# A second expert matrix split between a dense and a gathered product: 896 and 1152 columns instead of 1024 and 1024

## The chip, the cores and the metric

The kernel runs on one core of a Trainium2 chip. A core has five engines with instruction streams of their own: TensorE (PE, matrix products, with the loading of weights shown apart as PEld), VectorE (DVE), ScalarE (ACT), GpSimd (POOL) and SyncE (SP), which here only issues transfers. Sixteen DMA engines move data between the chip's memory (HBM) and the core's memory (SBUF); matrix products land in PSUM, eight banks of 512 fp32 numbers for each of 128 partitions. The metric is the device time of one execution in microseconds (us), the median of several; lower is better.

## What is computed

Two transformer blocks on 256 tokens of width 2048, in fp32. The change lies in the second block's expert layer. Each token gets 128 of 16384 experts with a weight each (eight heads, the sixteen best of each); expert e has a row of 2048 numbers in `expert_u` and one in `expert_v`:

```
def block(args):
    xb, ib, gb = args                 # tokens, their 128 expert indices, their 128 gates
    act = jax.nn.gelu(jnp.einsum('tkd,td->tk', expert_u[ib], xb))
    return jnp.einsum('tk,tkd->td', act * gb, expert_v[ib])
...
h = h + peer(rms_norm_2(h, ffn_norm_gain[i]), w_pq[i], sub_k1[i], sub_k2[i], expert_u[i], expert_v[i])
gate = jax.nn.sigmoid(rms_norm_2(h, ple_norm_gain[i]) @ w_ple_gate[i])
h = h + gate * (p[i] @ w_ple_proj[i])
```

## The kernel before

Every engine executes its instructions in the order in which the program writes them. That order comes out of a main line of code and of five lanes, generators that are stepped beside it: `lanes.step()` takes one step in each lane, `step_one(4)` one in lane 4 alone.

Weights come in chunks of 128 x 1024 numbers, 512 KB each, into four buffers `raw` (L335), issued on SP's queue in a fixed order. `next_chunk` releases the chunk just used, issues the load that takes its buffer, and steps the lanes once. Most weights are split into two parts by ACT (L349) and DVE (L350); the expert weights are used whole.

The expert layer has these pieces. First `u_rows` (lane 4) gathers, for each of 256 slots, the 128 rows of `expert_u` that the tokens ask for (two times 128 slots for two tiles of 128 tokens; L1663, 8 KB a row), and DVE multiplies them with the tokens and sums (L1703). The rows stand in seats of the slabs `rows`; with the second tile only four seats are used.

Then the product with `expert_v` is made in two ways, each for a part of its 2048 columns:

- Gathered, `w_vs`: `v_rows` (lane 4) gathers a row for each of 128 tokens per slot (256 gathers) into seats `vrow`, which are pieces of the first two `rows` slabs, and DVE multiplies by the slot's weight and adds into `sacc` in PSUM (L1838 for a tile's first slot, L1840 for the others). A step of the lane issues up to two gathers, if their seats are free, and writes one accumulation. After 128 slots ACT copies `sacc` out (L1847), and `turned` lets PE transpose it by blocks into the PSUM tile `tok` (L1815), from where DVE adds it to `x` (L1817).
- Dense, `w_vd`: a matrix G with one row for each of the 16384 experts and one column for each token holds the weights. `spots` builds it, eight tokens at a time, as products of two indicator matrices P and Q (L1762, L1794), which ACT copies out (L1745). Then 128 chunks of 128 experts are multiplied on PE (L1900) and summed in four PSUM banks `accv`. For the second tile of tokens the half with the lower experts is built before this loop (PSUM tile `sp`), the other half beside its first 62 chunks (PSUM tile `tok`).

The loop over the chunks takes two steps of lane 4 for each chunk: one inside `next_chunk`, one with `step_one(4)`. Ahead of the second stands a small copy on POOL that reads the chunk, so POOL goes on only when the chunk has landed:

```
for j in range(8):
    w, _ = next_block()
    if j == 0:
        G.tensor_copy(xb["beat"], w[:, 0:1])
        lanes.step_one(4)
    o = ps[j // 2][:, (j % 2) * T:(j % 2) * T + T]
    PE.matmul(o, w, gs_[k // 16][:, k % 16], ...)
```

Behind the loop the four banks are added to `x` (L1904), the blocks of `x` are squared and split (`x_block`), the projections `w_pp` and `w_pg` follow, and the result is stored.

Of the kernel before, what the change touches and what calls it, by code (L numbers as in the profile page):

```python
# [6 lines left out]
F32 = mybir.dt.float32  # L7
# [8 lines left out]
T = 256  # L16
D = 2048
DFF = 5632
NEG = -1.0e30
CH = 1024  # L20
GORD = [3, 2, 1, 0]
HORD = [0, 4, 1, 5, 2, 6, 3, 7]

# [40 lines left out]
def layout(i):  # L64

    a = {}
# [43 lines left out]
    a["w_pq"] = blocks(i["w_pq_2"][0])  # L110
    a["subk"] = np.ascontiguousarray(np.stack([i["sub_k1_2"][0], i["sub_k2_2"][0]], axis=1).transpose(3, 0, 1, 2)).reshape(128, 2048)
    a["w_u"] = np.ascontiguousarray(i["expert_u_2"][0])
    a["w_vd"] = np.ascontiguousarray(i["expert_v_2"][0][:, :CH])
    a["w_vs"] = np.ascontiguousarray(i["expert_v_2"][0][:, CH:])
    a["w_pg"] = blocks(i["w_ple_gate_2"][0])
    a["w_pp"] = blocks(i["w_ple_proj_2"][0])
    a["pt"] = np.ascontiguousarray(i["p_2"][0, 0].T.reshape(2, 128, T).transpose(1, 0, 2))
# [108 lines left out]
def program(tc, A, out, stage=99, dbg=None):  # L226
# [62 lines left out]
    def bank(p, name):  # L289
        return p.tile([128, 512], F32, name=name, tag="bank")  # L290
# [26 lines left out]
    if stage > 3:  # L317
        add("w_pq", split=False)
        whole.update(range(len(order), len(order) + 128))
        add_kout("w_vd", 128, 0)  # L320
    if stage > 4:
        add("w_pp"); add("w_pg")

# [1199 lines left out]
    def pair(name):  # L1523

        return pairs_[name].tile([128, 1024], F32, name=name, tag="pair")
# [190 lines left out]
    def spots(tt):  # L1716
# [50 lines left out]
        else:  # L1767

            for half in range(2):
                lo, p = half * 64, None  # L1770
                for n in range(16):
# [15 lines left out]
                            yield  # L1787
                    else:
                        G.tensor_mul(Pn, Pn, wT[:, ts][:, :, None].to_broadcast(narrow))
                    if half == 0 or n % 2 == 0:  # L1790
                        p = pair("tok" if half else "sp")
                    at = 0 if half == 0 else n % 2 * 512
                    for k in range(8):
                        PE.matmul(p[:, at + k * 64:at + k * 64 + 64], Q[:, k], P[:, k, 0:64], start=True, stop=True)  # L1794
                    if half:
                        yield
                    if half and n % 2:
                        put(range(4, 8), t0 - 8, p, 16)
                    elif not half:
                        put(range(4), t0, p[:, 0:512], 8)  # L1800
                    yield
                flags[("g", 1, half)] = True
        flags[("g", tt)] = True


    vrow = [t.rearrange("p n d -> p (n d)").rearrange("p (n d) -> p n d", n=4)[:, j] for t in rows_[:2] for j in range(4)]
# [12 lines left out]

    def v_rows():  # L1820
        while not flags.get("u"):
            yield
        m, busy = 0, {}
        sacc = None
        for n in range(256):
            tt, s = divmod(n, 128)
            for _ in range(4 if n == 0 else 1):
                for _ in range(2):
                    if m < 256 and m % 8 not in busy:
                        gather(vrow[m % 8], A["w_vs"], m)  # L1830
# [4 lines left out]
            r, w = vrow[n % 8], wv[:, tt, s:s + 1]  # L1835
# [5 lines left out]
            del busy[n % 8]  # L1841
            if s == 127:
                if tt:
                    t = vrow[1]
                else:
                    t = gs_["t"] = hip.tile([128, CH], F32, name="tok", tag="whi")
# [31 lines left out]
    for k in range(128):  # L1878
# [11 lines left out]
        if k == 84:  # L1890
            for j in range(2):
                part(pl[:, 0, j], pl[:, 1, j], pf[:, j], None)
        for j in range(8):
            w, _ = next_block()
            if j == 0:

                G.tensor_copy(xb["beat"], w[:, 0:1])
                lanes.step_one(4)
            o = ps[j // 2][:, (j % 2) * T:(j % 2) * T + T]
            PE.matmul(o, w, gs_[k // 16][:, k % 16], start=(k == 0 and j % 2 == 0), stop=k == 127, skip_group_check=True)  # L1900
    x, xh, xl = xb["x"], xb["h"], xb["l"]

    for i, q_ in enumerate(ps):
        V.tensor_add(x[:, 2 * i:2 * i + 2], x[:, 2 * i:2 * i + 2], q_.rearrange("p (k t) -> p k t", t=T))  # L1904
    for j in range(8):
        x_block(j, x, C("ple"), xh, xl)
    gt5 = xb["c"](4, T)
    pl = xb["p"]
# [4 lines left out]

    project(16, 2, (pl[:, 0], pl[:, 1]), pp_done)
    until("v")
    for j in range(8, 16):
        x_block(j, x, C("ple"), xh, xl)
    psum_close(3)
    accp, bgN = psum("accz", 4), psum("bgz", 1)
# [35 lines left out]
```

## Time and profile before

| | us |
|---|---|
| median of three runs | 2967.11 |
| lowest, highest | 2965.75, 2971.43 |
| profiled execution | 2963.08 |
| its span, first to last instruction | 2961.3 |
| PE, PEld, DVE busy | 2311.8, 2106.1, 1999.7 |
| ACT, POOL busy | 1191.2, 900.9 |

The profile is one execution. Busy times are sums over the span, so a share is a mean over stages with different limits; the stage that the change touches lies between about 2270 and 2870 us. PEclk is the granted clock of TensorE, 1.00 for 2.4 GHz and 0.50 for 1.2 GHz. The DMA share is the mean busy share of the sixteen DMA engines.

### The profile page before, as it was taken

The numbers are of one execution on the slowest core, as the hardware profiler recorded it, in microseconds if no ns is written. First come the engines' busy times: TensorE is split into PE (matmuls) and PEld (weight loads), VectorE is DVE, ScalarE is ACT, GpSimd is POOL, SyncE is SP. The second block draws the span as 40 slices with busy tenths as digits, with TensorE's granted clock in tenths as the row PEclk, the third lists the DMA queues.
The fourth block names the chain that finished last, engine by engine and source line by source line (L and its number), as shares of the span: only waits on it lengthen the run. The fifth ranks groups of instructions, "written<-read, shape, count | busy, mean of one in ns | idle before, by whom it ended". The sixth has DMA issues, their size and how long they took to land.

```text
span 2961.3 us, 39499 instructions
## 1 busy us (share of the span) xinstructions
PE 2311.8 (78%) x14635; PEld 2106.1 (71%) x14635; DVE 1999.7 (68%) x2615; ACT 1191.2 (40%) x2560; POOL 900.9 (30%) x1262
## 2 busy tenths in 40 slices
PE   8999999999999999999997200022222999999799
PEld 8887898888889999998986200011122988888689
DVE  5455666555556565656537999988998866666655
ACT  4355555444444454445411000058880444400043
POOL 3202215111111000331135543333334555555420
PEclk9999999999999999999998655555555799999999
DMA  6444455655655555543557799999997799999945
GB/s 221 153 128 122 134 158 180 196 188 187 197 187 190 185 180 184 172 151 109 182 201 279 291 407 422 422 397 408 415 415 317 265 403 404 395 401 409 366 148 166
DMA packets 174675, 765.11 MB, mean 258 GB/s; under 512 B 19585, under 2 KB 22049, under 8 KB 141201
## 3 DMA queue, kind: packets, MB, share of 16 engines
q1 hardware_dynamic: 99216, 353.83, 36.0%
q0 software_dynamic: 75264, 408.75, 34.5%
q8 instruction: 115, 1.88, 0.3%
q14 instruction: 80, 0.65, 0.1%
HBM read 757.77 MB, written 4.21 MB: 257 GB/s over the span
## 4 chain that ended last, share of the span: by engine, by line
PE 59%; DMA 12%; DVE 10%; issue 9%; POOL 8%; ACT 1%; another core or an unknown queue 0%; SPq 0%; POOLq 0%; DVEq 0%; ACTq 0%
PE acc L411 11%; PE acc L1900 7%; PE acc L386 6%; PE acc L388 6%; PE acc L387 6%; DMA rows<-w_vs,idx 6%; PE acc L412 6%; POOL rows L1663 5%; DMA rows<-w_u,idx 5%; DVE rows L1703 5%; PE acc L485 3%; PE acc L483 3%; PE acc L484 3%; PE sp L1794 1%; DMA raw<-w_vd 1%
## 5 line engine op out<-in xcount | busy, mean ns | idle before, releaser
L350 DVE TENSOR_TENSOR wlo<-raw,whi 128x1024 fp32r<-128x1024 f32 (+1 forms) x501 | 613.5, 1233 | 415.1 <-ACT whi L349 408.3
L349 ACT CAST whi<-raw 128x1024 fp32r<-128x1024 f32 (+1 forms) x501 | 519.7, 1042 | 380.2 <-PE acc L387 130.9
L1703 DVE SCALAR_TENSOR_TENSOR rows<-rows,yt 128x2048 f32<-128x2048 f32 x256 | 580.3, 2285 | 42.9 <-DMA rows<-w_u,idx 38.6
L1900 PE MATMUL acc<-G,raw 128*128 128x256 f32 x2048 | 457.3, 385 | 12.4 <-DMA raw<-w_vd 11.1
L1900 PEld LDWEIGHTS acc<-G,raw 128*128 128x128 f32 x2048 | 391.8, 193 | 71.7 <-DMA raw<-w_vd 17.0
L1840 DVE SCALAR_TENSOR_TENSOR sacc<-rows,sm,sacc 128x1024 f32<-128x1024 f32 x254 | 327.3, 1289 | 143.8 <-DMA rows<-w_vs,idx 127.4
L1663 POOL DMA_INDIRECT rows<-w_u,idx x256 | 244.2, 954 | 380.0 <-DVE rows L1703 274.8
L1663 POOL DMA_INDIRECT rows<-w_vs,idx x256 | 248.8, 972 | 149.6 <-DVE sacc L1840 81.7
L411 PE MATMUL acc<-xl,whi 128*128 128x512 f32 x704 | 248.2, 391 | 0.0
L411 PE MATMUL acc<-xh,whi 128*128 128x512 f32 x704 | 248.1, 391 | 0.0
L1762 PE MATMUL sp<-P,Q 128*128 128x128 f32 x256 | 60.2, 430 | 213.9 <-ACT P L1758 213.9
L1762 PEld LDWEIGHTS sp<-P,Q 128*128 128x128 f32 x256 | 55.8, 330 | 218.6 <-ACT P L1758 218.6
L564 POOL TENSOR_TENSOR acc_sq<-acc_sq,sq 128x256 f32<-128x256 f32 x63 | 57.0, 904 | 504.6 <-ACT sq L563 502.7
L485 PE MATMUL acc<-ring,wlo 128*128 128x256 f32 x704 | 199.3, 283 | 0.1
L483 PE MATMUL acc<-ring,whi 128*128 128x256 f32 x704 | 199.3, 283 | 0.1
L484 PE MATMUL acc<-ring,whi 128*128 128x256 f32 x704 | 199.2, 283 | 0.0
L412 PE MATMUL acc<-xh,wlo 128*128 128x256 f32 x704 | 197.2, 280 | 0.0
L412 PE MATMUL acc<-xl,wlo 128*128 128x256 f32 x704 | 197.1, 280 | 0.0
L1659 PE MATMUL yt<-keep,xg 128*128 128x128 f32 x32 | 5.6, 350 | 237.6 <-DVE rows L1703 237.1
L1191 POOL TENSOR_TENSOR hT<-cF 128x256 f32<-128x256 f32 x44 | 70.8, 1609 | 372.7 <-ACT whi L349 342.8
L1659 PEld LDWEIGHTS yt<-keep,xg 128*128 128x128 f32 x32 | 5.0, 184 | 238.1 <-DVE rows L1703 237.3
L386 PE MATMUL acc<-xh,whi 128*128 128x256 f32 x520 | 150.6, 290 | 3.2 <-ACT whi L349 1.8
(486 smaller groups left out, 5692.7 us busy)
## 6 DMA issues: line engine op xcount, KB each, us to landing
raw<-w_gu SPq DMA_DIRECT2D x176, 512.0 KB
raw<-w_vd SPq DMA_DIRECT2D x128, 512.0 KB
raw<-w_down SPq DMA_DIRECT2D x88, 512.0 KB
raw<-w_out SPq DMA_DIRECT2D x32, 512.0 KB
raw<-w_pq SPq DMA_DIRECT2D x32, 512.0 KB
raw<-w_pg SPq DMA_DIRECT2D x32, 512.0 KB
raw<-w_b SPq DMA_DIRECT2D x24, 512.0 KB
raw<-w_lat SPq DMA_DIRECT2D x18, 512.0 KB
```

Of the source, the lines that this page charges most:

```text
L349: S.copy(hi[j][:, a:b], raw[j][:, a:b])
L350: V.tensor_sub(lo[j][:, a:b], raw[j][:, a:b], hi[j][:, a:b].bitcast(F32))
L386: PE.matmul(ps, wh, xh, start=start, stop=False, **k)
L411: PE.matmul(ps, wh, xh.both(k), start=k == 0, stop=False, skip_group_check=True)
L412: PE.matmul(ps[:, :T], wl, xh[:, k], start=False, stop=k == kb - 1, skip_group_check=True)
L483: PE.matmul(o, wh, ah, start=(k == 0 and j % 2 == 0), stop=False, skip_group_check=True)
L484: PE.matmul(o, wh, al, start=False, stop=False, skip_group_check=True)
L485: PE.matmul(o, wl, ah, start=False, stop=(k == nk - 1), skip_group_check=True)
L1663: G.indirect_dma_start(dst, None, src, bass.IndirectOffsetOnAxis(ap=idx[:, tt, s:s + 1], axis=0))
L1703: V.scalar_tensor_tensor(r, r, 1.0, accT, op0=OP.mult, op1=OP.mult, accum_out=wv[:, tt, s:s + 1])
L1840: V.scalar_tensor_tensor(sacc, r, w, sacc, op0=OP.mult, op1=OP.add)
L1900: PE.matmul(o, w, gs_[k // 16][:, k % 16], start=(k == 0 and j % 2 == 0), stop=k == 127, skip_group_check=True)
```

## The change

The border between the two parts of `expert_v` moves by one block of 128 columns: the dense part has seven blocks (896 columns, `DV`), the gathered part nine (1152 columns, `SV`). What follows from it: a dense chunk is 448 KB and takes seven products; a gathered row is 4608 bytes instead of 4096; the two slabs hold six seats instead of eight; `sacc` takes three PSUM banks instead of two, and `tok` one instead of two. So the second half of G is copied out after every eight tokens instead of every sixteen, and the gathered part goes back into `x` in three groups of 4, 4 and 1 blocks through one bank.

```diff
-    a["w_vd"] = np.ascontiguousarray(i["expert_v_2"][0][:, :CH])
-    a["w_vs"] = np.ascontiguousarray(i["expert_v_2"][0][:, CH:])
+    a["w_vd"] = np.ascontiguousarray(i["expert_v_2"][0][:, :DV])
+    a["w_vs"] = np.ascontiguousarray(i["expert_v_2"][0][:, DV:])
...
-                    if half == 0 or n % 2 == 0:
-                        p = pair("tok" if half else "sp")
-                    at = 0 if half == 0 else n % 2 * 512
+                    p = bank(pairs_["tok"], "tok") if half else pair("sp")
...
-                    if half and n % 2:
-                        put(range(4, 8), t0 - 8, p, 16)
-                    elif not half:
-                        put(range(4), t0, p[:, 0:512], 8)
+                    put(range(4 * half, 4 * half + 4), t0, p[:, 0:512], 8)
...
-    vrow = [t.rearrange("p n d -> p (n d)").rearrange("p (n d) -> p n d", n=4)[:, j] for t in rows_[:2] for j in range(4)]
+    vflat = [t.rearrange("p n d -> p (n d)") for t in rows_[:2]]
+    vrow = [t[:, j * SV:j * SV + SV] for t in vflat for j in range(3)]
...
-        p = pair("tok")
-        for j in range(8):
-            PE.transpose(p[:, j * 128:j * 128 + 128], t[:, j * 128:j * 128 + 128], ident)
-        o = xb["x"][:, 8:16, tt * 128:tt * 128 + 128]
-        V.tensor_add(o, o, p.rearrange("p (k t) -> p k t", k=8))
+        for j0 in range(0, 16 - KV, 4):
+            n = min(4, 16 - KV - j0)
+            p = bank(pairs_["tok"], "tok")
+            for j in range(n):
+                b = t[j0 + j]
+                PE.transpose(p[:, j * 128:j * 128 + 128], b, ident)
+            o = xb["x"][:, KV + j0:KV + j0 + n, tt * 128:tt * 128 + 128]
+            V.tensor_add(o, o, p[:, :n * 128].rearrange("p (k t) -> p k t", k=n))
...
-                    if m < 256 and m % 8 not in busy:
-                        gather(vrow[m % 8], A["w_vs"], m)
-                        busy[m % 8] = m
+                    if m < 256 and m % 6 not in busy:
+                        gather(vrow[m % 6], A["w_vs"], m)
+                        busy[m % 6] = m
...
-                sacc = pair("sacc")
+                sacc = pairs_["sacc"].tile([128, 1536], F32, name="sacc", tag="sacc")[:, :SV]
...
-                S.copy(t, sacc)
+                S.copy(t, sacc[:, :CH])
+                S.copy(t2, sacc[:, CH:])
...
-        for j in range(8):
-            w, _ = next_block()
-            if j == 0:
-
-                G.tensor_copy(xb["beat"], w[:, 0:1])
-                lanes.step_one(4)
+        w, _ = next_chunk()
+
+        G.tensor_copy(xb["beat"], w[:, 0:1])
+        lanes.step_one(4)
+        for j in range(KV):
...
-    for j in range(8):
+    for j in range(KV):
         x_block(j, x, C("ple"), xh, xl)
```

The first place is on POOL, where the gathers of `w_vs` begin while `spots` builds the lower half of the second tile (P is multiplied by the weights between them; `rows_15106` and `rows_15107` are the two slabs). Before:

```order
L1789 TENSOR_TENSOR P<-P,acc_sq 128x8x64
L1663 DMA rows_15106<-w_vs,idx 128x1024 x2
L1789 TENSOR_TENSOR P<-P,acc_sq 128x8x64
L1663 DMA rows_15106<-w_vs,idx 128x1024 x2
L1789 TENSOR_TENSOR P<-P,acc_sq 128x8x64
L1663 DMA rows_15107<-w_vs,idx 128x1024 x2
L1789 TENSOR_TENSOR P<-P,acc_sq 128x8x64
L1663 DMA rows_15107<-w_vs,idx 128x1024 x2
L1789 TENSOR_TENSOR P<-P,acc_sq 128x8x64 x2
L1663 DMA rows_15106<-w_vs,idx 128x1024
```

And now:

```order
L1793 TENSOR_TENSOR P<-P,acc_sq 128x8x64
L1667 DMA rows_15106<-w_vs,idx 128x1152 x2
L1793 TENSOR_TENSOR P<-P,acc_sq 128x8x64
L1667 DMA rows_15106<-w_vs,idx 128x1152
L1667 DMA rows_15107<-w_vs,idx 128x1152
L1793 TENSOR_TENSOR P<-P,acc_sq 128x8x64
L1667 DMA rows_15107<-w_vs,idx 128x1152 x2
L1793 TENSOR_TENSOR P<-P,acc_sq 128x8x64 x3
L1667 DMA rows_15106<-w_vs,idx 128x1152
L1793 TENSOR_TENSOR P<-P,acc_sq 128x8x64
```

Six gathers go out ahead of the first accumulation instead of eight, in three pairs instead of four; from then on one follows each accumulation as before.

The second place is on PE, from the transposes of the first tile to those of the second and the chunks behind them (`tok<-keep` are transposes, `acc<-G,raw` the dense products). Before:

```order
L1900 MATMUL acc<-G_16316,raw 128x256 x24
L1815 MATMUL tok<-keep,tok 128x128 x8
L1900 MATMUL acc<-G_16317,raw 128x256 x128
L1900 MATMUL acc<-G_16318,raw 128x256 x128
L1900 MATMUL acc<-G_16319,raw 128x256 x128
L1900 MATMUL acc<-G_16320,raw 128x256 x64
L1815 MATMUL tok<-keep,rows_15106 128x128 x8
L1900 MATMUL acc<-G_16320,raw 128x256 x64
```

And now:

```order
L1903 MATMUL acc<-G_16316,raw 128x256 x21
L1818 MATMUL tok<-keep,tok 128x128 x8
L1818 MATMUL tok<-keep,rows_15106 128x128
L1903 MATMUL acc<-G_16317,raw 128x256 x112
L1903 MATMUL acc<-G_16318,raw 128x256 x112
L1903 MATMUL acc<-G_16319,raw 128x256 x112
L1903 MATMUL acc<-G_16320,raw 128x256 x56
L1818 MATMUL tok<-keep,rows_15106 128x128 x8
L1818 MATMUL tok<-keep,rows_15107 128x128
L1903 MATMUL acc<-G_16320,raw 128x256 x56
```

Every 128 products have become 112, and the transposes, which stand at the same chunks as before, are nine instead of eight.

The third place is on DVE, the last accumulations of the second tile and what follows them (`x<-x,tok` adds the transposed blocks). Before:

```order
L1840 SCALAR_TENSOR_TENSOR sacc<-rows_15106,sm,sacc 128x1024 x4
L1840 SCALAR_TENSOR_TENSOR sacc<-rows_15107,sm,sacc 128x1024 x4
L1840 SCALAR_TENSOR_TENSOR sacc<-rows_15106,sm,sacc 128x1024 x4
L1840 SCALAR_TENSOR_TENSOR sacc<-rows_15107,sm,sacc 128x1024 x4
L1817 TENSOR_TENSOR x<-x,tok 128x8x128
L350 TENSOR_TENSOR wlo<-raw,whi 128x1024 x2
L1904 TENSOR_TENSOR x<-x,acc 128x512 x4
```

And now:

```order
L1843 SCALAR_TENSOR_TENSOR sacc<-rows_15107,sm,sacc 128x1152 x3
L1843 SCALAR_TENSOR_TENSOR sacc<-rows_15106,sm,sacc 128x1152 x3
L1843 SCALAR_TENSOR_TENSOR sacc<-rows_15107,sm,sacc 128x1152
L1820 TENSOR_TENSOR x<-x,tok 128x4x128 x2
L1820 TENSOR_TENSOR x<-x,tok 128x128
L354 TENSOR_TENSOR wlo<-raw,whi 128x1024 x2
L1909 TENSOR_TENSOR x<-x,acc 128x512 x3
L1909 TENSOR_TENSOR x<-x,acc 128x256
```

One addition has become three, each of which reads the same PSUM bank; the accumulations are 1152 columns wide and go round six seats.

## Rows read from the trace of the kernel before

**Rows 1.** Windows: busy us and count of each engine, PEclk, DMA share, GB/s.

```profile
1800.00:1900.00 100.00, 0.00 (x0) 0.00 (x0) 94.11 (x83) 0.00 (x0) 38.15 (x41) 0.50 1.01 422
1950.00:2250.00 300.00, 60.22 (x256) 55.77 (x256) 272.37 (x237) 236.33 (x763) 111.84 (x119) 0.55 1.00 411
1950.00:2000.00 50.00, 11.35 (x48) 10.46 (x48) 46.02 (x41) 43.07 (x140) 19.32 (x21) 0.50 0.97 395
...
2340.00:2440.00 100.00, 100.00 (x516) 89.46 (x516) 70.83 (x59) 56.55 (x184) 53.10 (x77) 1.00 1.02 399
2440.00:2540.00 100.00, 96.86 (x487) 85.83 (x486) 66.20 (x55) 48.36 (x156) 50.59 (x73) 0.98 1.01 397
2540.00:2640.00 100.00, 99.34 (x488) 87.83 (x487) 64.91 (x53) 18.23 (x57) 54.36 (x77) 1.00 1.02 402
2640.00:2740.00 100.00, 96.36 (x435) 82.81 (x434) 67.21 (x54) 0.71 (x2) 54.88 (x80) 0.98 1.03 409
2340.00:2800.00 460.00, 446.95 (x2163) 391.38 (x2162) 309.12 (x250) 123.84 (x399) 243.07 (x349) 0.99 1.02 403
```

**Rows 2.** The chain that ended last, in order of time: start, us, what.

```profile
2333.05 6.01 PE acc L1900 x16
...
2341.21 13.87 PE acc L1900 x64
2355.08 1.73 PE tok L1794 x16
...
2492.09 13.46 DMA raw<-w_vd
...
2663.27 13.65 DMA rows<-w_vs,idx
...
2811.81 22.67 PE acc L1900 x96
2834.53 3.62 DMA raw<-w_pp
```

**Rows 3.** By form, 2340 to 2812, and the same lines by windows.

```profile
L1663 POOL DMA_INDIRECT rows<-w_vs,idx x230 | 220.8, 960 | 144.4 <-DVE sacc L1840 81.1 <-issue 45.7 <-DMA rows<-w_vs,idx 17.2
...
2340.00:2800.00 460.00, 22.76 (x118) 0.99 1.02 403
```

**Rows 4.** DMA, 1750 to 1900 and 2650 to 2790: packets, MB, share of 16 engines.

```profile
q0 software_dynamic: 8689, 63.26, 101.3%
...
q0 software_dynamic: 10479, 38.13, 68.3%
```

**Rows 5.** Single lines: ns min/median/max, first and last start, form.

```profile
L1840 DVE SCALAR_TENSOR_TENSOR sacc<-rows,sm,sacc x254: 1274/1289/1291, 2292.5 to 2807.4; 128x1024 f32<-128x1024 f32 x127
...
L1745 ACT COPY G<-tok x32: 372/384/403, 2356.8 to 2581.3; 128x256 f32<-128x256 f32 x32
...
L1904 DVE TENSOR_TENSOR x<-x,acc x4: 677/678/679, 2840.4 to 2842.2; 128x512 f32<-128x512 f32 x4
...
L1847 ACT COPY rows<-sacc x1: 1012/1012/1012, 2808.8 to 2808.8; 128x1024 f32<-128x1024 f32 x1
```

**Rows 6.** Windows of 10 us, columns as in the first group.

```profile
2310.00:2320.00 10.00, 10.00 (x49) 10.00 (x49) 8.83 (x10) 2.32 (x12) 6.08 (x6) 0.50 0.47 152
...
2340.00:2350.00 10.00, 10.00 (x53) 8.94 (x53) 9.76 (x9) 8.19 (x28) 4.33 (x7) 1.00 1.03 402
2490.00:2500.00 10.00, 10.00 (x56) 9.02 (x55) 4.90 (x5) 8.02 (x27) 4.18 (x6) 1.00 1.03 428
2690.00:2700.00 10.00, 7.90 (x30) 6.40 (x29) 6.45 (x5) 0.00 (x0) 5.32 (x8) 0.83 1.03 409
2750.00:2760.00 10.00, 8.54 (x39) 7.04 (x39) 6.25 (x5) 0.00 (x0) 5.17 (x7) 1.00 1.03 407
```

**Rows 7.** Timeline: start us, us, instruction, [idle before it and its releaser].

```profile
2282.44 3.68 PE L1794 MATMUL sp<-P,Q 128*128 128x64 f32 x16 [0.77 <-POOL P L1789]
...
2286.70 3.68 PE L1794 MATMUL sp<-P,Q 128*128 128x64 f32 x16 [0.59 <-POOL P L1789]
...
2591.84 1.22 DVE L1817 TENSOR_TENSOR x<-x,tok 128x1024 f32<-128x1024 f32 x1 [7.28 <-PE tok L1815]
...
2692.36 8.00 PE L1900 MATMUL acc<-G,raw 128*128 128x256 f32 x28 [2.10 <-DMA raw<-w_vd]
```

More of the change, by code (lines that the diff above doesn't have):

```diff
@@ L20 @@
 CH = 1024
+KV = 7
+DV = KV * 128
+SV = 2048 - DV
 GORD = [3, 2, 1, 0]
@@ L319, in program @@
         whole.update(range(len(order), len(order) + 128))
-        add_kout("w_vd", 128, 0)
+        for j in range(128):
+            order.append((A["w_vd"][j * 128:(j + 1) * 128], DV))
     if stage > 4:
@@ L1789, in spots @@
                         G.tensor_mul(Pn, Pn, wT[:, ts][:, :, None].to_broadcast(narrow))
-                    if half == 0 or n % 2 == 0:
-                        p = pair("tok" if half else "sp")
-                    at = 0 if half == 0 else n % 2 * 512
+                    p = bank(pairs_["tok"], "tok") if half else pair("sp")
                     for k in range(8):
-                        PE.matmul(p[:, at + k * 64:at + k * 64 + 64], Q[:, k], P[:, k, 0:64], start=True, stop=True)
+                        PE.matmul(p[:, k * 64:k * 64 + 64], Q[:, k], P[:, k, 0:64], start=True, stop=True)
                     if half:
                         yield
-                    if half and n % 2:
-                        put(range(4, 8), t0 - 8, p, 16)
-                    elif not half:
-                        put(range(4), t0, p[:, 0:512], 8)
+                    put(range(4 * half, 4 * half + 4), t0, p[:, 0:512], 8)
                     yield
@@ L1834, in v_rows @@
                     yield
-            r, w = vrow[n % 8], wv[:, tt, s:s + 1]
+            r, w = vrow[n % 6], wv[:, tt, s:s + 1]
             if s == 0:
-                sacc = pair("sacc")
+                sacc = pairs_["sacc"].tile([128, 1536], F32, name="sacc", tag="sacc")[:, :SV]
                 V.tensor_scalar(sacc, r, w, None, op0=OP.mult)
@@ L1840, in v_rows @@
                 V.scalar_tensor_tensor(sacc, r, w, sacc, op0=OP.mult, op1=OP.add)
-            del busy[n % 8]
+            del busy[n % 6]
             if s == 127:
[L1843 to L1846, printed above, removed]
-                S.copy(t, sacc)
+                t = vrow[1][:, :CH] if tt else hip.tile([128, CH], F32, name="tok", tag="whi")
+                t2 = vflat[tt][:, 3 * SV:3 * SV + SV - CH]
+                S.copy(t, sacc[:, :CH])
+                S.copy(t2, sacc[:, CH:])
+                t = [t[:, j * 128:j * 128 + 128] for j in range(8)] + [t2[:, j * 128:j * 128 + 128] for j in range(8 - KV)]
                 if tt:
@@ L1892, in program @@
                 part(pl[:, 0, j], pl[:, 1, j], pf[:, j], None)
-        for j in range(8):
-            w, _ = next_block()
-            if j == 0:
-                G.tensor_copy(xb["beat"], w[:, 0:1])
-                lanes.step_one(4)
+        w, _ = next_chunk()
+        G.tensor_copy(xb["beat"], w[:, 0:1])
+        lanes.step_one(4)
+        for j in range(KV):
             o = ps[j // 2][:, (j % 2) * T:(j % 2) * T + T]
-            PE.matmul(o, w, gs_[k // 16][:, k % 16], start=(k == 0 and j % 2 == 0), stop=k == 127, skip_group_check=True)
+            PE.matmul(o, w[:, j * 128:j * 128 + 128], gs_[k // 16][:, k % 16], start=(k == 0 and j % 2 == 0), stop=k == 127, skip_group_check=True)
     x, xh, xl = xb["x"], xb["h"], xb["l"]
+    st["blk"] = 8
     for i, q_ in enumerate(ps):
-        V.tensor_add(x[:, 2 * i:2 * i + 2], x[:, 2 * i:2 * i + 2], q_.rearrange("p (k t) -> p k t", t=T))
-    for j in range(8):
+        o = x[:, 2 * i:min(2 * i + 2, KV)]
+        V.tensor_add(o, o, q_.rearrange("p (k t) -> p k t", t=T)[:, :min(2, KV - 2 * i)])
+    for j in range(KV):
         x_block(j, x, C("ple"), xh, xl)
@@ L1915, in program @@
     until("v")
-    for j in range(8, 16):
+    for j in range(KV, 16):
         x_block(j, x, C("ple"), xh, xl)
```

## The prediction

> **What bounds the kernel now.** I read the profile from the whole to the stretch. The table by windows [rows 1] comes first: the last stage of the expert layer, from 2340 to 2800 us, is where both expert products run side by side, and there four of the engines could be the bound, so each has to be excluded or kept. DVE is busy 309 of 460 us, ACT 124, POOL 243: none of them. PE is busy 447 of 460, and the DMA engines are at a share of 1.02 with 403 GB/s. So two candidates are left, and they have to be separated by halves of the stage. The chain that ended last does this [rows 2]. Until 2492 it holds PE alone: four dense chunks of eight blocks (each product counts as two passes, so x64), 13.87 us, then the sixteen matmul passes that build the next eight tokens of the matrix G, 1.73 us, together 15.60 us or 3.90 us a chunk. After that, PE waits for a chunk, and from 2616 on the chain is gathers: a gather's landing (13.65 us), one accumulation on DVE, the next issue. There the window from 2640 to 2740 shows 409 GB/s at a share of 1.03, with PE at 96.4 of 100.
>
> The two halves run at nearly one pace because they are tied together. On POOL each chunk has a small copy (L1897) that waits for the chunk's landing, and two gathers (L1663) stand between two such copies; the chunk's buffer is free only once PE and that copy have read it. From 2340 to 2800 POOL issued 230 gathers and made 118 copies [rows 3], 1.95 gathers a chunk. Neither stream can run ahead of the other by more than its buffers: four for chunks, eight for gathered rows.
>
> So PE and DMA are almost equal bounds now. In bytes: 348 transfers (118 + 230) of 524,288 bytes are 182.5 MB; with the 2.1 MB reload of x and 0.26 MB for p it is 184.8 MB, and 403 GB/s for 460 us is 185.4 MB. The count explains what was moved, so the same count can be made for the changed kernel.
>
> **The change, part by part.**
>
> *PE.* A chunk keeps seven of eight blocks: 13.87/4 x 7/8 = 3.03 us instead of 3.47. With the G passes (1.73/4) the first half comes to 3.46 us a chunk, the second to 3.03. Over 118 chunks that is 51 us less work, and it moves PE well below the DMA. It gains time only as far as the DMA lets it, so I price it at nothing here; what hides it is the gathers.
>
> *DMA.* A dense chunk shrinks to 128 x 3584 = 458,752 bytes, a gather grows to 128 x 4608 = 589,824. The lockstep keeps 230 gathers to 118 chunks, so the stretch has to move 230 x 0.5898 + 118 x 0.4588 + 2.36 = 192.2 MB, 7.3 more than before. Two gathers fewer are under way when it begins (six seats instead of eight, the first piece of the order shows it), which adds 1.2 MB: 193.3 MB. The rate: 409 GB/s where only the DMA sets the pace, 397 to 402 in the three windows ahead of it, where PE held it back part of the time. Now PE has slack everywhere, so I take 406. 193.3/0.406 = 476 us, 16 more than 460. The ends are 409 (473 us, +13) and 397 (487 us, +27). A check by packets instead of bytes: 8,192-byte rows took 101.3% x 150 x 16 / 7,722 = 315 ns each, 4,096-byte rows 68.3% x 140 x 16 / 9,309 = 164 ns [rows 4] (packets counted as MB over row size, so the end marks are in the price). Between these two rows a byte costs 0.0368 ns, so a 4,608-byte row takes 183 and, on the same line, a 3,584-byte row 145: 2 x 183 + 145 = 511 against 492, 3.9% more for a chunk with its two gathers, against 4.2% by bytes. Nothing in the sizes makes up for the amount.
>
> *DVE.* One accumulation takes 1289 ns for 1024 columns [rows 5]; by the ratio at most 1450 for 1152. Two of them, 2.9 us, fit into a chunk's 4.0 us. Before the dense loop, in the 16 steps with one accumulation each, PE's G passes set the pace (10.00 us busy of 10, at 0.50 of the clock [rows 6]) while DVE is at 8.8 of 10, and 0.16 us more in each step of 3.7 us still fits. Without that cover it would be 16 x 0.16 = 2.6 us. ACT has twice as many copies of half the size (L1745, 384 ns each before [rows 5]): 32 x 0.384 us more at most, 12 us in a stretch where ACT idles 336.
>
> *POOL.* Its first steps of the stage hold two gathers each and set the pace: the G passes on PE start 4.26 us apart and wait for POOL's product, where they take 3.68 us themselves [rows 7]. Three such steps stand there now instead of four, up to 0.6 us less for the one, and the two gathers before the next product are gone: about -1 us.
>
> *The token-major half's way back.* Nine blocks go through one PSUM bank in groups of 4, 4, 1, and each group has to wait until DVE has added the one before (the second and third piece of the order). Behind these transposes on PE stand the remaining chunks. In the middle PE has to wait until DVE, at most a few rows behind, gets to the additions; the chunks' buffers and PE's slack of half a microsecond and more a chunk cover that, and without them it is the lag itself: before, DVE waited 7.28 us for PE there [rows 7]. I take +1. At the end nothing covers it: one more ACT copy of 128 columns (estimated at a quarter of the 1.01 us for 1024), two additions of 512 columns at 0.68, one more transpose: about +2 [rows 5]. Then the six chunks left run in 22.67 us [rows 2], by 7/8 in 19.84, and the 3.6 us wait for w_pp behind them is counted from PE's release of a buffer, so it moves along: -3. Later one block's square more lies after the stage and one less before it: 0.
>
> **Sum:** 16 - 1 + 1 + 2 - 3 = +15 us. The profiled execution took 2963.1, so 2978; the median of the three runs is 4.0 above it, and the forecast for it is 2967 + 15 = **2982 us**, slower by 0.5%. A comparison of this kernel can tell about 0.2%, 6 us, from no change.
>
> **The rivals.**
>
> *The DMA delivers more.* All terms but the stretch make -1, so the kernel is faster by more than 6 us if the stretch takes under 455 us, 193.3 MB at more than 425 GB/s; between 414 and 425 GB/s it is no change. For it: the gathers of u, with 8,192-byte rows, reach 422 [rows 1], and a 10 us window with the reload of x 428 [rows 6]. Against it: in the second half of u, with four seats, it is 411, and 409 is what the 4,096-byte rows reach; 4,608 lies an eighth of the way to 8,192. At 428 throughout, the stretch would take 452 us and the kernel 2967 - 8 - 1 = 2958. Faster 0.05, no change 0.07. The Trainium skill (DMA: Bandwidth & Descriptors, "Where 436 GB/s comes from") gives 435 GB/s as the ceiling of the ports into SBUF and says that HBM binds a core's loads near 358: by the first the stretch could take 444 us at best and the kernel 2950, by the second 540 us. The trace disagrees with the second (403 to 422 GB/s) and stays below the first.
>
> *The seats run short.* Six gathers of 0.59 MB are 3.5 MB under way at most, before 4.2. If that is too little to keep the engines full, the rate falls. Four seats of 1.05 MB held 411 on average and 395 in their worst 50 us [rows 1]. At 390 the stretch takes 496 us: 2967 + 36 - 1 = 3002. Chance 0.1.
>
> *PE's clock falls.* PE will wait in every chunk. At the half level, 1.2 GHz, a chunk of eight blocks took 6.01 us, the first of the loop [rows 2]; seven take 5.26, more than the DMA's 476/118 = 4.03. In the window from 2690 to 2700 PE had a wait of 2.1 us [rows 7] and the clock shows 0.83, while waits spread over 2750 to 2760, with PE busy 8.5 of 10, left it at 1.00 [rows 6]. If half of all chunks ran cold, they would average 4.15 us in the second half and 4.58 in the first: 58 x 0.55 + 60 x 0.12 = 39 us more, 3021. It decides from where 45% of the second half's chunks, or 26% of the first's, run cold. Against it: a cold PE has no gaps left, and the loop itself came back from 0.50 to 1.00 within its first chunk or two [rows 2, 6]. The Trainium skill (TensorE: Matmul & The Clock Gate, "HAM oscillation — how this bites in real kernels") warns of exactly this loop, bursts of matmuls between waits for DMA, which drop to the half clock each time; the rows above show it only for the long wait. Chance 0.04.
>
> **How the numbers follow.** The forecast, DMA-bound with 397 to 409 GB/s, has 0.74: +12 to +26, so 2979 to 2993. With seats 0.1, clock 0.04, no change 0.07, faster 0.05, slower has 0.88. The range that leaves out less than 2 in 10 is 2971 to 3004: below the forecast's own end into no change, above it to the rate of 390.
>
> **What would show it.** From 2340 on: 400 to 410 GB/s at a share above 1.0 for some 16 us longer, PE busy about 85% instead of 97% with waits for w_vd from the first chunks on, and the chain made of gathers from much earlier than 2616. Accumulations at 1.4 us. PE waiting for DVE between groups of transposes. The clock staying near 1.0. Wrong it would be if the GB/s rose past 420, or if the stretch's DMA share fell below 1.0, which means seats, PE or a wait that I priced at nothing.

## The result, and the profile after

| | before | after |
|---|---|---|
| median, us (six runs each, side by side) | 2966.43 | 2983.23 |
| lowest, highest | 2959.45, 2971.43 | 2980.74, 2990.49 |
| ratio, 95% interval | | 1.0056 [1.0038, 1.0075] |
| profiled execution | 2963.08 | 2982.12 |
| its span | 2961.3 | 2980.4 |

The changed kernel is slower by 0.56%, 16.6 us with an interval of 11 to 22; the forecast was 2982 us. The windows of the kernel after, columns as in [rows 1]:

```profile
2340.00:2440.00 100.00, 98.31 (x506) 86.81 (x505) 73.39 (x56) 59.80 (x202) 53.00 (x75) 1.00 1.02 409
2440.00:2540.00 100.00, 90.52 (x432) 77.97 (x431) 71.30 (x54) 50.04 (x168) 50.84 (x72) 0.95 1.02 411
2540.00:2640.00 100.00, 86.35 (x390) 74.17 (x389) 73.29 (x57) 20.44 (x70) 52.52 (x73) 0.90 1.02 403
2640.00:2740.00 100.00, 80.53 (x347) 63.65 (x345) 70.48 (x52) 0.71 (x2) 52.42 (x76) 1.00 1.02 409
2340.00:2800.00 460.00, 405.03 (x1881) 341.25 (x1879) 331.24 (x246) 131.00 (x442) 240.22 (x339) 0.97 1.02 408
2590.00:2600.00 10.00, 1.27 (x5) 0.88 (x6) 7.64 (x7) 0.00 (x0) 5.46 (x9) 0.60 1.01 400
2600.00:2610.00 10.00, 10.00 (x34) 8.34 (x35) 9.43 (x8) 0.00 (x0) 4.64 (x7) 0.71 0.95 353
```

PE is no longer a candidate for the bound: 405 of 460 us busy where [rows 1] has 447, and 80 of 100 in the window from 2640, yet the stage is longer. The DMA share is 1.02 as before, at 408 GB/s instead of 403. Apart from one place the sixteen DMA engines are what is full throughout these 460 us. The last two lines show that place, at 2600, and are needed further down.

The chain that ended last, of the kernel after, in order of time (start, us, what):

```profile
2350.51 7.99 DMA raw<-w_vd
...
2361.93 9.53 DMA rows<-w_vs,idx
...
2371.56 1.43 DVE sacc L1843
...
2827.60 1.02 ACT rows L1849
2828.66 1.13 PE tok L1818 x4
2829.82 0.70 DVE x L1820
2830.56 1.13 PE tok L1818 x4
2831.71 0.70 DVE x L1820
...
2832.99 20.61 PE acc L1903 x84
2853.66 3.66 DMA raw<-w_pp
```

In [rows 2] the first half of the stage was PE alone, and gathers came into the chain at 2616, with this line of the kernel before:

```profile
2616.23 14.93 DMA rows<-w_vs,idx
```

Now transfers are in it from 2350. Of the whole span, the chain gives PE 59% and DMA 12% before (first line), PE 52% and DMA 18% after:

```profile
PE 59%; DMA 12%; DVE 10%; issue 9%; POOL 8%; ACT 1%; another core or an unknown queue 0%; SPq 0%; POOLq 0%; DVEq 0%; ACTq 0%
PE 52%; DMA 18%; DVE 11%; issue 10%; POOL 8%; ACT 1%; SPq 0%; POOLq 0%; DVEq 0%; ACTq 0%
...
L1843 DVE SCALAR_TENSOR_TENSOR sacc<-rows,sm,sacc 128x1152 f32<-128x1152 f32 x254 | 361.2, 1422 | 134.4 <-DMA rows<-w_vs,idx 132.1
L1903 PE MATMUL acc<-G,raw 128*128 128x256 f32 x1792 | 416.9, 391 | 38.7 <-DMA raw<-w_vd 37.7
```

The two groups under them are the two consumers in the kernel after. DVE's 1.42 us for an accumulation has 134 us of idle time ahead of it in all, nearly all of it ended by a gather's landing; PE's products have 38.7, ended by chunks. Both wait for transfers, so neither sets the pace.

Where the difference lies can be cut out with three marks that both traces have. "Stage" below always means the time from the first dense product to ACT's copy of the second tile's sums.

| us | before | after | difference |
|---|---|---|---|
| last accumulation of u begins | 2267.9 | 2271.9 | +4.0 |
| from there to the first dense product | 65.2 | 64.3 | -0.9 |
| stage | 475.7 | 491.4 | +15.7 |
| ACT copy to the next dense product | 3.0 | 5.4 | +2.4 |
| six of the eight chunks left, until a buffer is free for w_pp | 22.7 | 20.6 | -2.1 |
| behind them | 126.8 | 126.7 | 0 |

The first row lies ahead of everything that the change touches: single executions vary there (the profiled ones of the experiments reach this mark between 2268 and 2288). So 15.1 of the 19.1 us between the two spans belong to the change, and the stage alone makes 15.7.

### The profile page after: what moved, and what is told of

Read it like the earlier page. It is cut to its first block, busy times and chain, and to the rows that moved or that the text cites. A ratio compares the mean times of both kernels' runs of the same rounds, so it can differ in the third digit from the quotient of the medians.

```text
span 2980.4 us, 39043 instructions
## 1 busy us (share of the span) xinstructions
PE 2281.3 (77%) x14381; PEld 2064.8 (69%) x14381; DVE 2035.5 (68%) x2619; ACT 1195.4 (40%) x2594; POOL 898.8 (30%) x1262
## 4 chain that ended last, share of the span: by engine, by line
PE 52%; DMA 18%; DVE 11%; issue 10%; POOL 8%; ACT 1%; SPq 0%; POOLq 0%; DVEq 0%; ACTq 0%
DMA rows<-w_vs,idx 12%; PE acc L415 10%; PE acc L390 6%; PE acc L392 6%; PE acc L391 6%; PE acc L416 5%; POOL rows L1667 5%; DMA rows<-w_u,idx 5%; DVE rows L1707 5%; PE acc L489 3%; PE acc L487 3%; PE acc L488 3%; PE sp L1796 1%; DVE sacc L1843 1%; PE acc L460 1%
## 5 line engine op out<-in xcount | busy, mean ns | idle before, releaser
L1843 DVE SCALAR_TENSOR_TENSOR sacc<-rows,sm,sacc 128x1152 f32<-128x1152 f32 x254 | 361.2, 1422 | 134.4 <-DMA rows<-w_vs,idx 132.1
L1903 PE MATMUL acc<-G,raw 128*128 128x256 f32 x1792 | 416.9, 391 | 38.7 <-DMA raw<-w_vd 37.7
L1903 PEld LDWEIGHTS acc<-G,raw 128*128 128x128 f32 x1792 | 345.0, 196 | 104.6 <-DMA raw<-w_vd 56.7
```

The source lines that it names most:

```text
L1903: PE.matmul(o, w[:, j * 128:j * 128 + 128], gs_[k // 16][:, k % 16], start=(k == 0 and j % 2 == 0), stop=k == 127, skip_group_check=True)
```

## The experiments

The theory: the stage moves at the pace of the DMA engines, whose time goes by bytes, and a block of columns costs twice as many bytes gathered as dense, because two gathers stand against one chunk. The rivals: the relief of PE gives something back or, with its gaps, costs something; six seats are too few; the new waits around the transposes make the difference. The medians are of four to twelve executions of each kernel; ratios are against the kernel before, run on the same chip. Three kernels leave out part of the result: `p1_seven_products` the eighth dense block, `p4_narrow_gather` the last 128 gathered columns, `p9_no_middle_turn` the first tile's gathered part; `p6_nine_products` adds the second block twice, and in `p3_eight_products` the extra product goes to a part of PSUM that nothing reads.

| kernel | from | median, us | ratio | stage, us | GB/s |
|---|---|---|---|---|---|
| before | | 2965.7 to 2967.6 | | 475.7 | 402 |
| after | | 2983.23 | 1.0056 | 491.4 | 408 |
| `p1_seven_products` | before | 2964.60 | 0.9987 | 469.8 | 408 |
| `p2_six_seats` | before | 2965.50 | 0.9996 | 474.1 | 406 |
| `p6_nine_products` | before | 2990.77 | 1.0085 | 494.9 | 382 |
| `p3_eight_products` | after | 2991.73 | 1.0086 | 492.7 | 407 |
| `p4_narrow_gather` | after | 2951.94 | 0.9943 | 458.0 | 401 |
| `p7_wide_chunks` | after | 3001.31 | 1.0119 | 507.5 | 410 |
| `p9_no_middle_turn` | after | 2979.64 | 1.0038 | 489.4 | 410 |
| `p8_five_seats` | after | 2987.35 | 1.0071 | 493.9 | 406 |
| `p5_four_seats` | after | 3065.16 | 1.0345 | 566.6 | 356 |

The rate is that of 450 us from 7 us behind the first dense product. The stage and the rate are from one execution each. The windows of the kernel before and of the kernel after, with which those of the experiments are compared:

```profile
2340.10:2790.10 450.00, 438.49 (x2125) 384.26 (x2125) 302.53 (x245) 123.74 (x398) 240.12 (x342) 0.99 1.02 402
2343.20:2793.20 450.00, 397.21 (x1844) 335.01 (x1844) 322.98 (x241) 127.90 (x431) 234.29 (x331) 0.97 1.02 408
```

**Fewer bytes, more bytes.** `p4_narrow_gather` is the kernel after with rows of 4096 bytes again, `p7_wide_chunks` the kernel after with chunks of 512 KB again; the seven products and six seats stay in both.

```diff
-    a["w_vs"] = np.ascontiguousarray(i["expert_v_2"][0][:, DV:])
+    a["w_vs"] = np.ascontiguousarray(i["expert_v_2"][0][:, DV:DV + CH])
...
-                        gather(vrow[m % 6], A["w_vs"], m)
+                        gather(vrow[m % 6][:, :CH], A["w_vs"], m)
```

> The changed kernel with gathers of 1024 of the 1152 columns (rows of 4096 bytes; the last 128 columns of the gathered part are not loaded, DVE reads what stands in the seat); every instruction stays. If bytes set the stage: 232 x 0.524 + 118 x 0.459 + 2.36 = 178.1 MB against 193.3, at 410 GB/s 434 us against 471, so some 37 us less than the changed kernel, ratio to before about 0.993; PE then needs 3.46 of 3.68 us a chunk in the first half and stays under the DMA. If seats, waits or the clock set it: within 10 us of the changed kernel.

```diff
-    a["w_vd"] = np.ascontiguousarray(i["expert_v_2"][0][:, :DV])
+    a["w_vd"] = np.ascontiguousarray(i["expert_v_2"][0][:, :CH])
...
-            order.append((A["w_vd"][j * 128:(j + 1) * 128], DV))
+            order.append((A["w_vd"][j * 128:(j + 1) * 128], CH))
```

> The changed kernel with the dense chunks loaded 1024 columns wide (512 KB; the eighth block's columns are loaded and not used); all other work as it is, the result untouched. If bytes set the stage, on whichever queue: 118 x 0.0655 = 7.7 MB more, at 410 GB/s 19 us more than the changed kernel, ratio to before 1.010 to 1.014. If it is the gathers alone that set the stage (their seats, their size, POOL and DVE around them) and the chunks' loads are hidden beside them: as the changed kernel, ratio 1.004 to 1.007.

The narrow gather takes 33.4 us out of the stage and 31.3 us out of the median, the wide chunks put 16.1 us into the stage and 18 into the median (0.63% by the ratios); 37 and 19 us had been expected. Their windows, of 450 us each, first the narrow gather:

```profile
2347.30:2797.30 450.00, 408.14 (x1925) 346.98 (x1924) 346.14 (x257) 127.66 (x431) 246.82 (x354) 0.97 1.02 401
```

and the wide chunks:

```profile
2345.90:2795.90 450.00, 396.83 (x1798) 336.91 (x1798) 312.32 (x233) 127.93 (x431) 226.66 (x321) 0.94 1.02 410
```

In both, the engines' share stays at 1.02 and the rate within 3% of the 408 of the kernel after; what changes is how much has to be moved. The stage of the narrow gather moved 399 GB/s x 458.0 us = 182.7 MB, that of the kernel after 404 x 491.4 = 198.5 MB. Bytes on the gathers' queue and bytes on the chunks' queue count alike, and in both directions. Counted by transfers, 237 gathers and 123 chunks with 128 rows and 512 bytes a row, the first edit takes 15.5 MB out and the second puts 8.1 MB in: 2.0 to 2.2 us for each MB on either queue, a little less than the stage's mean of 2.5 (491.4 us for 198.5 MB). DVE is busier with the narrow gather (346 of 450 us against 323 in the kernel after) though no accumulation was taken out or added: its 1152-wide accumulations are merely packed closer. So the longer accumulations did not set the pace either.

**PE's work, taken away and put back.** `p1_seven_products` leaves the eighth product out of the kernel before; every transfer stays.

```diff
-            PE.matmul(o, w, gs_[k // 16][:, k % 16], start=(k == 0 and j % 2 == 0), stop=k == 127, skip_group_check=True)
+            if j < 7:
+                PE.matmul(o, w, gs_[k // 16][:, k % 16], start=(k == 0 and j % 2 == 0), stop=k == 127, skip_group_check=True)
...
```

> The kernel before with seven products a chunk instead of eight (the eighth block of the dense part is left out of the sum and of x); all transfers as before. If bytes set the stage: the stretch still moves 184.8 MB, and at the 410 GB/s that the changed kernel reached that is 451 us instead of 460; with 2 us from the six chunks at the end, about 11 us less than before, ratio 0.996, PE busy under 90%, GB/s up from 403 to 408 to 410. If PE's work set the stage: 0.43 us less in each of 118 chunks, 30 to 51 us less, ratio 0.983 to 0.990.

`p3_eight_products` puts an eighth product back into the kernel after; the transfers stay as they are there.

```diff
-        for j in range(KV):
+        for j in range(8):
...
-            PE.matmul(o, w[:, j * 128:j * 128 + 128], gs_[k // 16][:, k % 16], start=(k == 0 and j % 2 == 0), stop=k == 127, skip_group_check=True)
+            PE.matmul(o, w[:, j % KV * 128:j % KV * 128 + 128], gs_[k // 16][:, k % 16], start=(k == 0 and j % 2 == 0), stop=k == 127, skip_group_check=True)
```

> The changed kernel with an eighth product a chunk (a repeat of the first block, into the unused half of the fourth bank; the result is untouched). If bytes set the stage: PE needs 3.90 us a chunk beside the G passes and 3.47 behind them, under the DMA's 4.0, so the stretch stays; the six chunks at the end take 2 to 2.5 us more: ratio to before 1.0055 to 1.008. If PE's gaps and what they do to its clock cost the changed kernel time: filling them makes it faster than the changed kernel by 3 us or more, ratio at most 1.0045, and the clock shows fewer windows under 1.00.

`p6_nine_products` gives PE more than the transfers need: in the kernel before, the second block's product is made twice.

```diff
             PE.matmul(o, w, gs_[k // 16][:, k % 16], start=(k == 0 and j % 2 == 0), stop=k == 127, skip_group_check=True)
+            if j == 1:
+                PE.matmul(o, w, gs_[k // 16][:, k % 16], start=False, stop=k == 127, skip_group_check=True)
```

> The kernel before with nine products a chunk (the second block's is added twice, so x is not the reference's there); all transfers as before. If PE and DMA are near equal bounds before: PE becomes the bound, 13.87/4 x 9/8 = 3.90 us a chunk, 4.33 with the G passes, so 62 x 4.33 + 60 x 3.90 = 502 us against 476, with 3 us at the end: some 25 to 30 us more, ratio 1.008 to 1.010, GB/s down to 380 to 390. If PE had room for a ninth product beside the transfers: 3 us more at the end alone, ratio 1.000 to 1.002.

Windows of the seven products:

```profile
2352.40:2802.40 450.00, 406.90 (x1918) 343.80 (x1918) 306.37 (x248) 124.87 (x398) 243.69 (x348) 0.99 1.03 408
```

of the eight products with the new transfers:

```profile
2347.60:2797.60 450.00, 428.69 (x2069) 371.59 (x2069) 322.41 (x240) 127.14 (x431) 234.01 (x330) 0.99 1.02 407
```

and of the nine:

```profile
2359.90:2459.90 100.00, 100.00 (x504) 89.10 (x503) 66.25 (x55) 52.12 (x168) 46.76 (x67) 1.00 0.97 362
2459.90:2559.90 100.00, 100.00 (x512) 89.31 (x511) 61.28 (x52) 44.56 (x146) 48.11 (x70) 1.00 1.00 384
2559.90:2659.90 100.00, 100.00 (x500) 88.95 (x499) 59.16 (x48) 24.62 (x78) 49.95 (x71) 1.00 0.96 359
2659.90:2759.90 100.00, 100.00 (x465) 88.04 (x464) 66.94 (x54) 0.71 (x2) 54.46 (x78) 1.00 1.03 409
```

With nine products PE is at 100 of 100 in each window, the rate falls to between 359 and 384 GB/s as long as the passes for G stand beside the chunks, and the kernel is slower by 0.85%, 25 us: one more product is all it takes to make PE the bound. With seven, PE is at 407 of 450 us and the transfers run at 408 GB/s, but the kernel gains only 0.13%, 4 us with an interval of 0 to 7. That is less than the 11 us that I had expected of it; in the traces its stage is 5.9 us shorter. With eight products over the new transfers the kernel is 0.3% slower than the kernel after, 9 us by the ratios, whose intervals (1.0038 to 1.0075 and 1.0066 to 1.0105) overlap; that is just above what was expected. The two traces show 3.8 us up to the last dense product, 1.3 in the stage and 2.5 behind it, where the last eight chunks run with nothing beside them. So the idle time of PE in the kernel after costs nothing: filling it makes the kernel slower, not faster.

**Fewer seats.** `p2_six_seats` is the kernel before with six of its eight seats; `p8_five_seats` and `p5_four_seats` are the kernel after with five and four of its six.

```diff
-                    if m < 256 and m % 8 not in busy:
-                        gather(vrow[m % 8], A["w_vs"], m)
-                        busy[m % 8] = m
+                    if m < 256 and m % 6 not in busy:
+                        gather(vrow[m % 6], A["w_vs"], m)
+                        busy[m % 6] = m
...
-            r, w = vrow[n % 8], wv[:, tt, s:s + 1]
+            r, w = vrow[n % 6], wv[:, tt, s:s + 1]
...
```

> The kernel before with six seats for gathered rows instead of eight, columns as before. If bytes set the stage: two gathers of 0.52 MB fewer under way at its beginning, 1 MB or 2.6 us, less 1 us for POOL's shorter beginning: ratio 1.000 to 1.002, GB/s as before (403). If the seats cost what the change cost: 10 us or more, ratio 1.003 to 1.006, GB/s lower.

```diff
-                    if m < 256 and m % 6 not in busy:
-                        gather(vrow[m % 6], A["w_vs"], m)
-                        busy[m % 6] = m
+                    if m < 256 and m % 4 not in busy:
+                        gather(vrow[m % 4], A["w_vs"], m)
+                        busy[m % 4] = m
...
-            r, w = vrow[n % 6], wv[:, tt, s:s + 1]
+            r, w = vrow[n % 4], wv[:, tt, s:s + 1]
...
```

> The changed kernel with four seats for gathered rows instead of six, all else as it is. If bytes set the stage and four gathers of 0.59 MB with the chunks beside them still keep the DMA engines full: two gathers fewer under way at its beginning (1.2 MB, 3 us) and 1 us less at POOL's beginning, ratio to before 1.005 to 1.008 with 408 to 410 GB/s. If the seats are near their limit with six: GB/s falls below 400, 12 us or more on top, ratio 1.010 or higher.

The same edit with 5 for 4:

> The changed kernel with five seats for gathered rows: 2.95 MB under way at most, between the 2.36 of four seats (356 GB/s, ratio 1.0345) and the 3.54 of six (408 GB/s, ratio 1.0056). If the DMA engines stay full down to some amount under way and six seats lie well above it: 400 GB/s or more, ratio 1.006 to 1.012. If six seats lie just above that amount: 375 to 390 GB/s, ratio 1.015 to 1.025.

From eight to six seats costs nothing that can be measured (0.9982 to 1.001), and the trace has 406 GB/s with PE at full work:

```profile
2359.10:2809.10 450.00, 439.21 (x2134) 383.05 (x2134) 303.40 (x246) 124.44 (x398) 241.99 (x344) 1.00 1.02 406
```

From six to five costs 2.5 us of stage, with medians 4 us apart and intervals that overlap. Five seats:

```profile
2339.00:2789.00 450.00, 396.06 (x1831) 333.82 (x1831) 321.46 (x240) 127.91 (x431) 233.67 (x329) 0.97 1.02 406
```

From six to four costs 75 us of stage and 82 us of the median. Four seats, the same stretch, and from the DMA view of 2650 to 2790 the rate in forty slices and the queues (packets, MB, share of 16 engines), with the same slices of the kernel after behind them:

```profile
2345.40:2795.40 450.00, 370.76 (x1640) 313.65 (x1640) 282.46 (x213) 128.12 (x431) 204.09 (x289) 0.91 0.97 356
```

```profile
GB/s 327 401 396 409 410 397 301 334 378 269 385 366 378 332 400 291 391 404 304 352 413 353 312 355 403 298 356 372 369 372 341 365 374 353 396 363 382 409 384 271
...
q0 software_dynamic: 8811, 36.02, 71.1%
q1 hardware_dynamic: 4556, 14.54, 26.6%
...
GB/s 409 415 403 409 411 405 411 410 413 408 402 409 413 408 407 415 409 410 413 413 403 411 413 408 415 412 405 406 414 410 407 408 414 408 415 406 409 412 408 411
```

With four seats the rate swings between 269 and 413 GB/s, with six it stays between 402 and 415. So the rival exists, but it begins below five seats; the six of the kernel after stand on flat ground, one seat above the last that holds the rate.

**The way back in the middle.** `p9_no_middle_turn` is the kernel after without the transposes and additions of the first tile.

```diff
-                    lanes.add(0, turned(t, 0, 8))
+                    pass
```

> The changed kernel without the first tile's way back (nine transposes and three additions in the middle of the loop, so the first 128 tokens lack the gathered part). If PE's 9 us of waits for DVE there are covered by its slack and the chunks' buffers: 0 to 3 us less than the changed kernel, ratio 1.0045 to 1.0060. If they stand in the way of the transfers: 6 to 10 us less, ratio 1.002 to 1.0035.

Its ratio is 1.0038 [1.0025, 1.0052], between the two cases expected, against the 1.0056 of the kernel after: 5 us by the ratios, with intervals that overlap, and 2.0 us of stage in one trace each. The timeline of PE in the kernel after shows the wait itself (start, us, instruction, and in brackets the idle time before it):

```profile
2597.94 1.11 PE L1818 MATMUL tok<-keep,tok 128*128 128x128 f32 x4 [8.21 <-DVE x L1820]
```

PE stood for 8.2 us and freed no chunk buffer, and POOL stood 3.5 us for DVE before its gather at 2602; in the window from 2600 the share fell to 0.95 and the rate to 353 GB/s (above). In the kernel without the transposes, whose stage began 10 us later, the windows read:

```profile
2540.00:2640.00 100.00, 89.75 (x396) 77.07 (x396) 73.09 (x54) 26.53 (x90) 52.75 (x75) 0.91 1.02 409
2600.00:2610.00 10.00, 6.79 (x31) 5.63 (x30) 8.46 (x7) 0.00 (x0) 6.01 (x10) 0.97 1.01 401
2610.00:2620.00 10.00, 10.00 (x41) 8.52 (x41) 6.88 (x5) 0.00 (x0) 4.53 (x7) 0.86 1.03 413
```

409 instead of 403 GB/s over 100 us is 0.6 MB, or 1.5 us. So of 8.2 us of wait most was covered, and the trace shows some 2 us left for the whole way back; whether it is 2 or 5 the runs don't settle. But not all of this is new. The kernel before has such a place too:

```profile
2590.00:2600.00 10.00, 10.00 (x52) 8.87 (x51) 7.98 (x7) 0.00 (x0) 3.08 (x4) 1.00 1.02 387
2600.00:2610.00 10.00, 10.00 (x49) 8.79 (x48) 8.14 (x7) 0.00 (x0) 8.27 (x12) 1.00 0.98 370
```

There it was DVE that stood 7.28 us for PE [rows 7], and POOL 7.74 us for DVE's next accumulation. Against 409 GB/s these two windows lack 0.61 MB, and those of the kernel after (400 and 353) lack 0.65. The way back costs about the same in both, with the wait moved from DVE to PE; by these two traces the change adds some 0.1 us here. No run left the way back out of the kernel before.

## Why the prediction was right

**DMA, +16.** Right, in sign and size: the stage grew by 15.7. The lockstep held: from the first dense product to the ACT copy POOL issued 237 gathers to 123 chunk copies in the kernel after, 235 to 123 in the kernel before. By the windows of the stage, before and after, its bytes rose from 399 x 475.7 = 189.8 MB to 404 x 491.4 = 198.5, by 8.7, where the step had 8.5 (193.3 - 184.8):

```profile
2333.10:2808.80 475.70, 453.81 (x2184) 396.85 (x2184) 321.04 (x260) 130.51 (x420) 249.12 (x359) 0.98 1.01 399
2336.20:2827.60 491.40, 422.26 (x1945) 354.68 (x1945) 353.96 (x262) 134.64 (x453) 252.37 (x361) 0.96 1.01 404
```

The price of a packet was right too. The DMA view of the kernel after, 2650 to 2790:

```profile
q0 software_dynamic: 10160, 41.55, 73.9%
q1 hardware_dynamic: 4931, 15.72, 28.4%
```

By the way of [rows 4], a 4,608-byte row took 73.9% x 140 x 16 / 9,017 = 184 ns and a 3,584-byte row 28.4% x 140 x 16 / 4,386 = 145 ns; the line between two other sizes had given 183 and 145. The rate came out at 408 over the 460 us, 2 above the value chosen and inside its ends. `p4_narrow_gather` and `p7_wide_chunks` show that bytes are the cause.

**PE's relief, nothing.** Nearly right. Of the 460 us PE idled 55 instead of 13, and the stage became longer all the same, so the work that it lost turned into idle time; its waits for chunks are 37.7 us of the page's row above. What its relief can have given back is at most what the rate gained: 402 to 408 GB/s in the traces. `p1_seven_products` has the same 408 with PE's work cut and all else as before, which speaks for PE; `p2_six_seats` has 406 with PE at full work, which speaks for the variation of single executions. By the ratio of `p1_seven_products` it is between 0 and 7 us, and within that it stays open.

**POOL -1, end +2, last six chunks -3.** Measured -0.9, +2.4 and -2.1. The six chunks are not the last, as the step has it: eight are left in both kernels, and the sixth frees the buffer for w_pp. They took 20.61 us instead of the 19.84 of the step. The windows of the kernel after show where the rest is, in TensorE's clock:

```profile
2830.00:2835.00 5.00, 3.57 (x11) 2.75 (x12) 1.48 (x3) 0.00 (x0) 0.00 (x0) 0.50 0.00 0
2835.00:2840.00 5.00, 5.00 (x18) 4.16 (x17) 0.00 (x0) 0.00 (x0) 0.00 (x0) 0.71 0.11 19
2840.00:2845.00 5.00, 5.00 (x24) 4.39 (x24) 0.00 (x0) 0.00 (x0) 0.37 (x2) 1.00 0.48 168
```

PE comes out of 12.9 us of idle time, then stops twice for DVE between its groups of transposes, and the granted clock is at the lower level (0.50, 1.2 GHz) until 2835 and back at 1.00 only from 2840, seven us after the chunks began. In the kernel before, with its eight transposes in one piece, the chunks began at 2811.8 and the clock was at 1.00 from 2817. The step scaled the 22.67 us by 7/8, the time at the lower clock with the rest, and left the stops out.

**The middle, +1.** The new wait was foreseen, and it came: PE stood 8.2 us for DVE. But the step priced it alone. DVE's old wait for PE, 7.28 us, went away with it, and with that a loss of bytes of the same size (0.61 MB before, 0.65 after); what the change adds in the middle is about 0.1 us by one trace of each kernel. The term was small, so the sum hardly suffered.

**DVE, ACT, nothing.** Right. An accumulation took 1.42 us where at most 1.45 was allowed. ACT's copies became 64 of 282 ns; their busy time, in which copies overlap, rose from 9.6 to 12.4 us, 2.8 us more where at most 12 were allowed:

```profile
L1745 ACT COPY G<-tok 128x256 f32<-128x256 f32 x32 | 9.6, 386 | 114.7 <-PE tok L1794 93.8 <-PE acc L1900 21.0
L1749 ACT COPY G<-tok 128x128 f32<-128x128 f32 x64 | 12.4, 282 | 31.7 <-PE tok L1796 31.7
```

**The rivals.** *The DMA delivers more* fell: no window of 100 us is above 411 GB/s. The Trainium skill's two figures for it (DMA: Bandwidth & Descriptors, "Where 436 GB/s comes from") stand to the kernel after as to the kernel before: 403 to 411 GB/s is above its 358 for HBM and below its 435 for the ports. *The seats* are a true mechanism at the wrong place: 390 GB/s was put on six seats, while six and five give 408 and 406, and four give 356. *PE's clock* fell in places, deepest around the wait of 8.2 us: 0.60 in the window that holds most of it, 0.71 behind it. It also fell behind a wait of 4.07 us for a chunk and behind one of 1.70 us for ACT (start, us, instruction, idle time before it; then the windows):

```profile
2458.20 3.09 PE L1796 MATMUL tok<-P,Q 128*128 128x64 f32 x16 [1.70 <-ACT P L1789]
2502.23 8.00 PE L1903 MATMUL acc<-G,raw 128*128 128x256 f32 x28 [4.07 <-DMA raw<-w_vd]
...
2460.00:2470.00 10.00, 10.00 (x38) 8.56 (x38) 6.97 (x6) 6.32 (x20) 5.30 (x8) 0.71 1.02 410
2500.00:2510.00 10.00, 7.77 (x28) 6.41 (x28) 7.14 (x6) 0.00 (x0) 4.19 (x6) 0.83 1.03 411
```

Over the 100 us from 2640, in which PE was busy 80.5 us and waited again and again for a chunk, up to 2.27 us at a time, it was 1.00. Over the 460 us it was 0.97; the stage of `p3_eight_products`, at 0.99, is no shorter, so this cost nothing here. The Trainium skill (TensorE: Matmul & The Clock Gate, "HAM oscillation — how this bites in real kernels") tells of a loop whose every wait for DMA brings the lower clock; the waits of its example are longer than most of those here, so it is not "exactly this loop", as the prediction calls it. The wait of 4.07 us agrees with it, and those up to 2.27 us from 2640 on brought no drop. The price of this rival was too low: the 6.01 us that it takes for a chunk at the half level lie in a window at 0.61 on average (2330 to 2340 of the kernel before), and it leaves the passes for G at full clock, although sixteen of them took 3.68 us at 0.50 [rows 7] against 1.73 [rows 2]. With twice the 3.03 us of seven products and these 3.68 us, half of the chunks cold would have cost about 100 us instead of 39 (an estimate).

All points named as signs were there: 403 to 411 GB/s at a share above 1.0, transfers in the chain from 2350, accumulations of 1.4 us, PE waiting for DVE between groups of transposes, the clock at 0.97. PE was busy 88% of the 460 us where 85 was said. The end of the sum agrees better than its terms deserve: 4.0 us of the difference between the profiled executions is none of the change's, the medians are 16.8 us apart with an interval of 11 to 22, and the errors of two small terms cancel: the middle was put 1 us too high, the six chunks 1 us too low.

## What to carry to other kernels

Where two streams are tied together and the DMA share is above 1.0, count bytes for each step of the lockstep. A move of work that takes time off a nearly full engine and adds bytes costs the bytes where the DMA engines are full, since the engine's relief becomes waiting. A new wait is priced together with the wait that it replaces: here PE's 8.2 us took the place of DVE's 7.28, at the same loss of bytes. Ask of "nearly equal bounds" with two kernels, one that takes work from the engine and one that takes bytes from the DMA: here an eighth of PE's products, taken from the kernel before, gave 4 us (0 to 7), and a ninth of the gathered bytes, taken from the kernel after, 31. Buffers for transfers can be cut for free down to an edge, and the edge has to be found by a run, since the rates of eight, six and five seats don't show that it is near.

## What was not expected of the hardware

- **The edge of the seats.** Six seats of 0.59 MB gave 408 GB/s, five 406, four 356. The second tile of u, with four seats of 1.05 MB, had held 411 [rows 1]; so four gathers as such are not too few, and in this stage 2.9 MB of seats were enough where 2.4 MB were not. Why it falls off so steeply there isn't shown: DVE's and POOL's turn-round is part of the time in which a seat is empty of a transfer.
- **A busy DMA engine isn't a delivering one.** With four seats the share was 0.97 at 356 GB/s, and a gathered row took 71.1% x 140 x 16 / 7,817 = 204 ns of an engine instead of 184. A chunk's row stayed at 147 (26.6% x 140 x 16 / 4,057) against 145. The share fell by 5%, the rate by 13%.
- **The clock with short waits.** At 80.5 us busy of 100, in pieces between waits for chunks of up to 2.27 us, the granted clock was 1.00 in each 10 us from 2640 to 2740. Behind single waits of 1.70 us (above) and 2.1 us [rows 7] it was 0.71 and 0.83; so the length of the last wait alone doesn't tell.
